# Gate rows of a dense PEER phase: groups of 16 blocks loaded in quarters, and the first eight blocks' rows of the third tile copied within SBUF

## The chip, the core and the metric

The kernel runs on one core of a Trainium2 chip. The metric is the device time of one execution in microseconds (us); before the change the median of 3 runs is 1922.52 us (1922.35 to 1923.98).

## What is computed

One inference step of a one-layer decoder on 576 tokens (512 of a prompt, 8 x 8 of a sample group) of width 1024: a mixer (an S5 state-space group and an RWKV-7 group), then PEER, a retrieval from 16384 experts of one neuron each. The change touches PEER alone:

```python
q = (xb @ w_q).reshape(PEER_BLOCK, PEER_HEADS, 2, PEER_HALF)
s1 = einsum('thd,hnd->thn', q[:, :, 0], k1); s2 = einsum('thd,hnd->thn', q[:, :, 1], k2)
v1, i1 = top_k(s1, 16); v2, i2 = top_k(s2, 16)
sc, pos = top_k(v1[..., :, None] + v2[..., None, :], 16)      # 8 heads x 16 experts per token
gate = softmax(sc)
act = gelu(einsum('thkd,td->thk', u_tab[idx], xb), approximate=False)
out = einsum('thk,thkd->td', gate * act, v_tab[idx])
```

## The kernel before

The tokens lie in five tiles, ORDER = (1, 2, 3, 0, 4); four have 128 tokens, tile 4 has 64. Each goes through front and back (the mixer, L1228 is its output projection), select (the queries, 64 matmuls `pas` with wq at L1268 in each half, and the products with the keys at L1284) and pick (the top-16 searches on DVE, L1304 to L1356). PEER's experts are then applied in two ways.

**Gathers, tiles 0 and 4.** POOL fetches each token's rows of u_tab and v_tab by indirect DMA (L1444, tile gr), DVE multiplies and adds (L1449 to scr, L1459 to acc). run() deals three such steps out to each dense block.

**Dense, tiles 1, 2 and 3 (384 tokens).** All 16384 experts are computed in 128 blocks of 128. For a block b, ublock() loads ur (512 KB), splits it into uh (ACT, L1512) and ul (DVE, L1513), and makes pd with 24 matmuls (L1516). dense() takes the Gelu of pd to wf (ACT, L1597), multiplies wf by the block's gate row (DVE, L1599), splits that into wh (ACT, L1602) and wl (DVE, L1603), loads vr (512 KB, L1611), splits it into vh (ACT, L1614) and vl (DVE, L1615), and adds into six PSUM banks with 18 matmuls po (L1619). dh and dl (L1551, L1552) are the split of the tokens, made once ahead.

**The gate rows.** For an expert that a token has not picked the gate is 0. gbuild(), woven with select and pick, makes the gate matrix for one dense tile in 8 steps of 16 tokens: for 4 tokens at a time (a group) two tiles ab are written (ACT L1490 and L1491 or DVE L1493; ACT L1496 or POOL L1498), four matmuls put their product into PSUM (L1501; par, pag, pah are the banks) and ACT copies that to Gst, 128 x 2048 (L1502). Gst is written to a buffer Gd in device memory, 1 MB for each of the 24 steps (L1504). From there loadG() in dense() (L1571) reads the rows of GBL = 8 blocks into a tile Gr, of which there are two: 16 tokens of 8 blocks are 512 bytes on end, so a load is 24 x 128 pieces of 512 bytes, 1.5 MB. There are 16 such loads.

All these loads and the writes of Gd are issued by SP, one after the other, on one queue; POOL's gathers are on another. The program is put in order by a scheduler ahead of time: each engine runs its instructions in a fixed order, and a DMA can be put ahead of where the code names it (issue_after).

Of the kernel before, what the change touches and what calls it, by code (L numbers as in the profile page):

```python
# [6 lines left out]
F32 = mybir.dt.float32  # L7
# [6 lines left out]
OP = mybir.AluOpType  # L14
# [164 lines left out]
class Kernel:  # L179
    DENSE = (1, 2, 3)  # L180
    ORDER = (1, 2, 3, 0, 4)
    TG = 16
    GBL = 8
    RATE = 3.0
    WS5, WAD, WS6, WA6, WD = 3.0, 0.0, 1.0, 1.0, 0.3
    PB = {"r": 3, "s": 3, "h": 1, "g": 1}
    UX, UWT, AB2 = 0, 0.5, 15
    UG = True
    UO = -100000
    PO, GO, SO, RO, FO = {}, {}, {4: 4000}, {}, {}  # L190
# [4 lines left out]
    GB = 5  # L195
# [1275 lines left out]
    def gbuild(self, d):  # L1471
        V, S, G, T, SY = self.nc.vector, self.nc.scalar, self.nc.gpsimd, self.nc.tensor, self.nc.sync
        iob = self.iota[:, None, :].to_broadcast([128, 4, 128])
        n = self.TG
        gp, nb = (self.gp2, self.AB2) if d == 2 and self.AB2 else (self.gp, self.AB)
        for tg in range(128 // n):
            Gst = self.gs.tile([128, 128, n], F32, name="Gst")
            for q in range(n // 4):
                t0 = d * 128 + tg * n + q * 4

                def bc(t):
                    return t[:, t0:t0 + 4, None].to_broadcast([128, 4, 128])
                oh = gp.tile([128, 128, 4], BF16, name="oh", bufs=self.OHB)
                B = gp.tile([128, 4, 128], F32, name="ab", bufs=nb)
                A = gp.tile([128, 4, 128], F32, name="ab", bufs=nb)
                self.gv = V.tensor_tensor(oh, self.io4, self.dib[:, None, t0:t0 + 4].to_broadcast([128, 128, 4]), op=OP.is_equal)  # L1486
                oh = oh.rearrange("p n t -> p t n")
                if q % 4 in self.BA:
                    for t in range(4):
                        S.activation(B[:, t], self.iota, AF.Abs, bias=self.dix[:, 0, t0 + t:t0 + t + 1], scale=-1.0)  # L1490
                    S.activation(B, B, AF.Relu, bias=1.0, scale=-1.0)  # L1491
                else:
                    self.gv = V.tensor_tensor(B, iob, bc(self.dix[:, 0]), op=OP.is_equal)  # L1493
                if q % 4 in self.AA:
                    for t in range(4):
                        S.activation(A[:, t], oh[:, t], AF.Copy, scale=self.dix[:, 1, t0 + t:t0 + t + 1])  # L1496
                else:
                    G.tensor_tensor(A, oh, bc(self.dix[:, 1]), op=OP.mult)  # L1498
                pg = self.ps([128, 4, 128], self.GR[d][(tg * n // 4 + q) % len(self.GR[d])])
                for t in range(4):  # L1500
                    T.matmul(pg[:, t, :], B[:, t, :], A[:, t, :], start=True, stop=True)  # L1501
                S.copy(Gst[:, :, 4 * q:4 * q + 4], pg.rearrange("p t n -> p n t"))  # L1502
                yield
            SY.dma_start(self.Gd[d * (128 // n) + tg], Gst.rearrange("p n t -> p (n t)"))  # L1504

    def ublock(self, b, pa, pool):
# [7 lines left out]
        for k in range(KB):  # L1514
            for i, (u, h) in enumerate(((uh, dh), (uh, dl), (ul, dh))):
                nc.tensor.matmul(pa, u[:, k, :], h[:, k, :], start=(k == 0 and i == 0), stop=(k == KB - 1 and i == 2))  # L1516

    def open_dense(self):
        S, V, SY = self.nc.scalar, self.nc.vector, self.nc.sync
        N = 128 * len(self.DENSE)  # L1520
        sc = self.sd = Scope(self.tc)
        kw = dict(reuse_waits="tile")
        dq = sc.pool("dq", **kw)
        self.ud = sc.pool("ud", **kw)
        if self.EU:
            self.ue = sc.pool("ue", **kw)
        if self.ED:
            self.dp = sc.pool("dp", 1, **kw)
        self.sh = Scope(self.tc)
        self.hf = self.sh.pool("hf", **kw).tile([128, KB, N], F32, name="hf")  # L1530
        if self.AB2:
            self.gp2 = self.sh.pool("gp2", **kw)
        ua = self.sh.pool("ua", **kw)
        self.ua = []
        for b in range(self.UX):
            t = ua.tile([128, KB, 128], F32, name="ua%d" % b)
            SY.dma_start(t, self.I["u_t"][b])
            self.ua.append(t)
        self.dh = dq.tile([128, KB, N], F32R, name="dh")
        self.dl = dq.tile([128, KB, N], F32R, name="dl")  # L1540
        self.wu = []
        for d, ti in enumerate(self.DENSE):
            sl = slice(128 * d, 128 * d + 128)
            SY.dma_start(self.hf[:, :, sl], self.h2d[ti].rearrange("p (k t) -> p k t", k=KB))

    def dense(self):
# [3 lines left out]
        N = 128 * nd  # L1550
# [15 lines left out]
                po = pso.tile([128, 512], F32, name="po%d%d" % (d, n))  # L1566
                outs.append(po)

        def loadG(g):
            t = dp.tile([128, N // TG, GBL, TG], F32, name="Gr", bufs=2)  # L1570
            SY.dma_start(t.rearrange("p g n t -> p g (n t)"),  # L1571
                         self.Gd[:, :, g * GBL * TG:(g + 1) * GBL * TG].rearrange("g p x -> p g x"))
            return t

        def first(b):
            if b < ux:
# [9 lines left out]

        with self.tc.issue_after(self.kld.ins):
            pa = first(0)
            G1 = loadG(0)
        for b in range(128):  # L1590
            if b % GBL == 0:
                Gr = G1
            if b % GBL == self.GPF and b + GBL < 128:
                with self.tc.issue_after(self.kld.ins):
                    G1 = loadG(b // GBL + 1)
            wf = pa if b < ux else dp.tile([128, N], F32, name="wf", bufs=2)
            S.activation(wf, pa, AF.Gelu)  # L1597
            w3 = wf.rearrange("p (g t) -> p g t", t=TG)
            V.tensor_tensor(w3, w3, Gr[:, :, b % GBL, :], op=OP.mult)  # L1599
            wh = dp.tile([128, N], F32R, name="wh", bufs=2)  # L1600
            wl = dp.tile([128, N], F32R, name="wl", bufs=2)
            S.copy(wh, wf)  # L1602
# [24 lines left out]
    def run(self, stop=None):  # L1627
# [48 lines left out]
        if stop == "mix":  # L1676
            weave(tc, (pk, 1.0, True))
        else:
            dense, gs = self.dense(), self.gathers()
            n = m = 0.0  # L1680
            for b, r in enumerate(dense):
                m += self.PW
                while m >= 1 and pk:
                    m -= 1
                    with tc.issue_after(self.gv.ins):
                        live = next(pk, 0)
                    if live == 0:
                        pk = None
                        self.sx.close()
                if b >= self.FB:  # L1690
                    if b == self.FB:
                        fl = self.open_finish()
                    with tc.issue_after(self.vld.ins):
                        next(fl, None)
                n += self.RATE * r * 128 / (128 - 0.5 * len(self.wu))
                with tc.issue_after(self.mark):
                    while n >= 1:
                        next(gs, None)
                        n -= 1
            for _ in gs:  # L1700
                pass
            self.sp.close()
            self.sf.close()
        if stop == "mix":
            self.sx.close()
            self.sh.close()
# [28 lines left out]
```

## Time and profile before

| | |
|---|---|
| median of 3 runs | 1922.52 us |
| the profiled execution, and its span | 1922.74 us, 1921.0 us |
| PE busy | 1772.8 us (92%) |
| DVE busy | 1508.1 us (79%) |
| ACT, POOL busy | 801.0 us (42%), 683.0 us (36%) |
| mean granted TensorE clock | 0.964 |
| share of the chain that ended last: PE | 62% |

The profile is of one execution. "Busy" is a share of the span; the chain of waits goes back from the last instruction to whatever released each step. The dense blocks begin at 804.5 us and the last block's po ends near 1898 us. Each block has 24 matmuls pd and 18 matmuls po.

### The profile page before, as it was taken

The page shows a single profiled execution, that of the slowest core. Times are in us where ns is not written, and L with a number is a line of the kernel's source. Part 1 is how long each engine was busy: PE and PEld are TensorE (multiplying, and loading weights), DVE is VectorE, ACT ScalarE, POOL GpSimd, SP SyncE. Part 2 cuts the span into 40 slices and gives each one's busy share as a digit, 9 for nine tenths or more (in the row PEclk, how much of TensorE's full clock was granted, in tenths as well). Part 3 has the DMA queues.
Part 4 walks back from the last instruction along what each step waited for, and adds up shares of the span by engine and source line. Part 5 has one row for each costly group of instructions (what it writes and reads, how often), then busy time and mean ns, then how long its engine had stood idle before and what let it go on. Part 6 is the DMA issues. An engine that isn't in the chain of part 4 may idle for free.

```text
span 1921.0 us, 32712 instructions
## 1 busy us (share of the span) xinstructions
PE 1772.8 (92%) x12299; PEld 1527.8 (80%) x12299; DVE 1508.1 (79%) x3073; ACT 801.0 (42%) x1466; POOL 683.0 (36%) x540
## 2 busy tenths in 40 slices
PE   8899987988879897889999999999999999999994
PEld 5699645757558676778999988899998999999993
DVE  7968324495996977789888877788888878888998
ACT  4232515535674677833333333433333333333332
POOL 0000101000351333334554444355445445444554
PEclk9999999989889898989999999999999999999998
DMA  8524654644345585589999998899999999999985
GB/s 328 159 87 105 202 179 145 205 138 151 122 150 195 193 296 210 221 297 333 370 340 340 350 356 313 295 374 342 343 355 317 347 340 343 331 342 349 331 318 190
DMA packets 203230, 513.82 MB, mean 267 GB/s; under 512 B 26232, under 2 KB 88824, under 8 KB 198976
## 3 DMA queue, kind: packets, MB, share of 16 engines
q1 hardware_dynamic: 147488, 309.34, 46.8%
q0 software_dynamic: 55584, 202.40, 28.7%
q8 instruction: 96, 1.57, 0.3%
q14 instruction: 62, 0.51, 0.1%
HBM read 470.89 MB, written 39.62 MB: 266 GB/s over the span
## 4 chain that ended last, share of the span: by engine, by line
PE 62%; DVE 10%; ACT 2%; DMA 1%; issue 1%; POOL 1%; POOLq 0%; DVEq 0%; ACTq 0%; SPq 0%
PE po L1619 27%; PE pd L1516 27%; PE pas L1268 3%; DVE oh L1486 1%; PE par L1501 1%; DVE ab L1493 1%; DMA Gr<-Gd 1%; PE pas L1228 1%; PE pag L1501 1%; PE pah L1501 1%; PE par L997 0%; DVE vals L1304 0%; DVE idxu L1305 0%; DVE idxu L1308 0%; DVE t2s L1306 0%
## 5 line engine op out<-in xcount | busy, mean ns | idle before, releaser
L1444 POOL DMA_INDIRECT gr<-v_tab,ei x192 | 261.0, 1359 | 274.6 <-DVE acc L1459 233.5
L1444 POOL DMA_INDIRECT gr<-u_tab,ei x192 | 251.6, 1310 | 274.0 <-DVE scr L1449 250.4
L1516 PE MATMUL pd<-dh,uh 128*128 128x384 f32 x1024 | 343.8, 336 | 4.8 <-ACT wf L1597 4.8
L1516 PE MATMUL pd<-dh,ul 128*128 128x384 f32 x1024 | 343.8, 336 | 0.0
L1516 PE MATMUL pd<-dl,uh 128*128 128x384 f32 x1024 | 343.2, 335 | 0.0
L1512 ACT CAST uh<-ur 128x1024 fp32r<-128x1024 f32 x128 | 134.5, 1050 | 276.7 <-PE pd L1516 264.3
L1459 DVE SCALAR_TENSOR_TENSOR acc<-gr,act,acc 128x1024 f32<-128x1024 f32 x190 | 243.2, 1280 | 2.3 <-DMA gr<-v_tab,ei 0.5
L1619 PE MATMUL po<-vl,wh 128*128 128x512 f32 x768 | 239.0, 392 | 0.6 <-DVE vl L1615 0.6
L1619 PE MATMUL po<-vh,wl 128*128 128x512 f32 x768 | 236.8, 390 | 0.0
L1449 DVE SCALAR_TENSOR_TENSOR scr<-gr,h 128x1024 bf16<-128x1024 f32 x192 | 235.1, 1224 | 1.4 <-DMA gr<-u_tab,ei 0.2
L1602 ACT CAST wh<-wf 128x384 fp32r<-128x384 f32 x128 | 65.8, 515 | 364.8 <-PE po L1619 348.0
L1513 DVE TENSOR_TENSOR ul<-ur,uh 128x1024 fp32r<-128x1024 f32 x128 | 156.5, 1223 | 78.2 <-ACT uh L1512 78.0
L1619 PE MATMUL po<-vh,wh 128*128 128x512 f32 x768 | 202.2, 398 | 15.2 <-ACT wh L1602 7.7
L1516 PEld LDWEIGHTS pd<-dh,uh 128*128 128x128 f32 x1024 | 192.3, 188 | 11.1 <-ACT wf L1597 5.8
L1516 PEld LDWEIGHTS pd<-dl,uh 128*128 128x128 f32 x1024 | 192.2, 188 | 6.0 <-issue 0.8
L1516 PEld LDWEIGHTS pd<-dh,ul 128*128 128x128 f32 x1024 | 192.1, 188 | 0.4
L1619 PEld LDWEIGHTS po<-vh,wh 128*128 128x128 f32 x768 | 141.8, 189 | 43.3 <-ACT vh L1614 12.8
L1615 DVE TENSOR_TENSOR vl<-vr,vh 128x1024 fp32r<-128x1024 f32 x128 | 156.2, 1220 | 22.0 <-ACT vh L1614 21.9
L1619 PEld LDWEIGHTS po<-vl,wh 128*128 128x128 f32 x768 | 144.5, 189 | 33.1 <-DVE vl L1615 1.4
L1619 PEld LDWEIGHTS po<-vh,wl 128*128 128x128 f32 x768 | 144.2, 188 | 31.2
L1498 POOL TENSOR_TENSOR ab<-oh,dix 128x512 f32<-128x512 bf16 x72 | 88.8, 1240 | 176.7 <-DVE oh L1486 68.9
L1614 ACT CAST vh<-vr 128x1024 fp32r<-128x1024 f32 x128 | 134.4, 1050 | 21.2 <-DMA vr<-v_tab 15.3
(471 smaller groups left out, 2976.2 us busy)
## 6 DMA issues: line engine op xcount, KB each, us to landing
ur<-u_t SPq DMA_DIRECT2D x128, 512.0 KB
vr<-v_tab SPq DMA_DIRECT2D x128, 512.0 KB
Gd<-Gst SPq DMA_DIRECT2D x24, 1024.0 KB
Gr<-Gd SPq DMA_DIRECT2D x16, 1536.0 KB
wo<-w_out SPq DMA_DIRECT2D x40, 512.0 KB
wq<-w_q SPq DMA_DIRECT2D x40, 512.0 KB
wt<-w_ada SPq DMA_DIRECT2D x32, 512.0 KB
wr<-w_in SPq DMA_DIRECT2D x18, 512.0 KB
```

The source lines that it names most:

```text
L1444: G.indirect_dma_start(out=r, out_offset=None, in_=I[tab], in_offset=bass.IndirectOffsetOnAxis(ap=ei[:, k:k + 1], axis=0))
L1449: V.scalar_tensor_tensor(scr, r, 1.0, h2, op0=OP.mult, op1=OP.mult, accum_out=act[:, k:k + 1])
L1459: V.scalar_tensor_tensor(acc, r, act[:, k:k + 1], acc, op0=OP.mult, op1=OP.add)
L1498: G.tensor_tensor(A, oh, bc(self.dix[:, 1]), op=OP.mult)
L1501: T.matmul(pg[:, t, :], B[:, t, :], A[:, t, :], start=True, stop=True)
L1512: nc.scalar.copy(uh, ur)
L1513: self.mark = nc.vector.tensor_tensor(ul, ur, uh.bitcast(F32), op=OP.subtract).ins
L1516: nc.tensor.matmul(pa, u[:, k, :], h[:, k, :], start=(k == 0 and i == 0), stop=(k == KB - 1 and i == 2))
L1602: S.copy(wh, wf)
L1614: S.copy(vh, vr)
L1615: V.tensor_tensor(vl, vr, vh.bitcast(F32), op=OP.subtract)
L1619: T.matmul(outs[2 * d + n], w[:, d * 128:(d + 1) * 128], v[:, n * 512:(n + 1) * 512], start=(b == 0 and i == 0), stop=(b == 127 and i == 2))
```

## The change

GBL goes from 8 to 16: a tile of gate rows now holds 16 blocks, so the 16 tokens of 16 blocks are 1024 bytes on end. Two large tiles, GA and GB, take turns (128 x 6144 numbers each). GA is opened before the third dense tile's gbuild, and the tiles ab of that gbuild go from 15 to 13. GB is opened when pick has ended. The first 16 blocks' rows are in GA, in two halves of 8 blocks. G0, blocks 0 to 7: for dense tiles 1 and 2 a DMA of 1 MB (in the first step of the third tile's gbuild), for the third tile 8 copies of 128 x 128 by DVE from Gst. G8, blocks 8 to 15: a load of 1.5 MB in 512-byte pieces. All later groups come in four loads of 6 x 128 pieces of 1024 bytes (768 KB).

```diff
-    GBL = 8
+    GBL = 16
-    UX, UWT, AB2 = 0, 0.5, 15
+    UX, UWT, AB2 = 0, 0.5, 13
...
                 S.copy(Gst[:, :, 4 * q:4 * q + 4], pg.rearrange("p t n -> p n t"))
                 yield
+            if d == 2:
+                V.tensor_copy(self.G0[:, d * (128 // n) + tg], Gst[:, 0:8, :])
+                if tg == 0:
+                    self.loadG(self.G0, 0, 8, 0, d * (128 // n))
             SY.dma_start(self.Gd[d * (128 // n) + tg], Gst.rearrange("p n t -> p (n t)"))
...
+    def loadG(self, t, b0, nb, g0, g1):
+        self.nc.sync.dma_start(t[:, g0:g1].rearrange("p g n t -> p g (n t)"),
+                               self.Gd[g0:g1, :, b0 * self.TG:(b0 + nb) * self.TG].rearrange("g p x -> p g x"))
...
+        self.GA = sc.pool("g0", 1, **kw).tile([128, N * self.GBL], F32, name="GA")
+        self.G0, self.G8 = (t.rearrange("p (g n t) -> p g n t", n=8, t=self.TG)
+                            for t in (self.GA[:, :8 * N], self.GA[:, 8 * N:]))
...
+        Gr, r0, plan = self.G0, 0, {2: (self.G8, 8, 8, 0, ng)}
...
             pa = first(0)
-            G1 = loadG(0)
         for b in range(128):
-            if b % GBL == 0:
-                Gr = G1
-            if b % GBL == self.GPF and b + GBL < 128:
+            if b == 8:
+                Gr, r0 = self.G8, 8
+            elif b and b % GBL == 0:
+                Gr, r0 = (GA, GB)[b // GBL % 2], b
+            if b == 11:
+                GB = self.GB_.rearrange("p (g n t) -> p g n t", n=GBL, t=TG)
+                for i in range(4):
+                    plan[11 + i] = GB, 16, GBL, ng // 4 * i, ng // 4 * (i + 1)
+            if b >= 16 and b % GBL == 0 and b + GBL < 128:
+                for i in range(4):
+                    plan[b + 2 + 2 * i] = (GA, GB)[(b // GBL + 1) % 2], b + GBL, GBL, ng // 4 * i, ng // 4 * (i + 1)
+            if b in plan:
                 with self.tc.issue_after(self.kld.ins):
-                    G1 = loadG(b // GBL + 1)
+                    self.loadG(*plan[b])
...
-            V.tensor_tensor(w3, w3, Gr[:, :, b % GBL, :], op=OP.mult)
+            V.tensor_tensor(w3, w3, Gr[:, :, b - r0, :], op=OP.mult)
```

Line numbers in the changed kernel are higher by 4 from gbuild's write on (Gd<-Gst L1508, ur L1513, uh L1516, pd L1520, loadG L1523), by 17 in dense() (wf L1614 and L1616, wh L1619, wl L1620, vr L1628, vh L1631, po L1636).

The change moves instructions. SP's order where the dense blocks begin, before:

```order
L1504 DMA Gd<-Gst 128x2048
L1509 DMA ur<-u_t 128x1024
L1571 DMA Gr<-Gd 128x24x128 x2
L1611 DMA vr<-v_tab 128x1024
L1509 DMA ur<-u_t 128x1024 x2
L1611 DMA vr<-v_tab 128x1024
```

and now (the first row stands earlier, between two loads of wq in the last tile's select; the second is the last write of Gd):

```order
L1523 DMA GA<-Gd 128x16x128
...
L1508 DMA Gd<-Gst 128x2048
L1513 DMA ur<-u_t 128x1024
L1523 DMA GA<-Gd 128x24x128
L1628 DMA vr<-v_tab 128x1024
L1513 DMA ur<-u_t 128x1024 x2
L1523 DMA GB<-Gd 128x6x256 x4
L1628 DMA vr<-v_tab 128x1024
```

Before, both first loads of gate rows stand behind the last write of Gd. Now only the second half of GA does, and the four quarters of GB follow three loads later, ahead of block 3's vr.

SP's order and, under it, ACT's order at the load that follows block 31's wf, before:

```order
L1611 DMA vr<-v_tab 128x1024
L1509 DMA ur<-u_t 128x1024
L1571 DMA Gr<-Gd 128x24x128
L1611 DMA vr<-v_tab 128x1024
L1509 DMA ur<-u_t 128x1024
```

```order
L1602 CAST wh<-wf 128x384
L1614 CAST vh<-vr 128x1024
L1597 ACTIVATE wf<-pd 128x384
L1512 CAST uh<-ur 128x1024
```

and now:

```order
L1628 DMA vr<-v_tab 128x1024
L1513 DMA ur<-u_t 128x1024
L1523 DMA GB<-Gd 128x6x256 x4
L1628 DMA vr<-v_tab 128x1024
L1513 DMA ur<-u_t 128x1024
```

```order
L1619 CAST wh<-wf 128x384
L1614 ACTIVATE wf<-pd 128x384
L1631 CAST vh<-vr 128x1024
L1516 CAST uh<-ur 128x1024
```

The four quarters, which the code names two blocks apart, stand in a row, with the next vr (block 31's) behind them. On ACT the Gelu of block 34 has moved ahead of block 31's vh; on PE, likewise, block 35's pd has moved ahead of block 31's po. Four quarters in a row stand behind block 31, 47, 63, 79 and 95; two and two stand behind blocks 7 and 15. At 47 PE's order is not turned in this way.

PE's order around the last tile's queries (pas<-t4s,wq) and key products, before:

```order
L1268 MATMUL pas<-t4s,wq 128x128 x32
L1501 MATMUL pag<-ab 128x128
L1268 MATMUL pas<-t4s,wq 128x128 x32
L1284 MATMUL pas<-keys,t4s 128x128 x8
L1501 MATMUL pag<-ab 128x128 x3
L1501 MATMUL par<-ab 128x128 x2
L1284 MATMUL pas<-keys,t4s 128x128 x8
L1501 MATMUL par<-ab 128x128 x2
```

and now:

```order
L1268 MATMUL pas<-t4s,wq 128x128 x32
L1501 MATMUL par<-ab 128x128 x4
L1501 MATMUL pag<-ab 128x128 x3
L1268 MATMUL pas<-t4s,wq 128x128 x8
L1501 MATMUL pag<-ab 128x128
L1501 MATMUL pah<-ab 128x128 x4
L1501 MATMUL par<-ab 128x128 x7
L1268 MATMUL pas<-t4s,wq 128x128 x24
L1284 MATMUL pas<-keys,t4s 128x128 x8
L1501 MATMUL par<-ab 128x128 x5
L1284 MATMUL pas<-keys,t4s 128x128 x8
```

Between the last key product and the first pd there were 90 matmuls of gbuild (22.5 groups of four); now there are 68 (17 groups), and the others stand among the queries. The split dh of the tokens on ACT and dl on DVE are also put later than before, dl into a pick.

## Rows read from the trace of the kernel before

**Rows 1.** The page: busy engines, DMA queues, and the chain's shares by line.

```profile
PE 1772.8 (92%) x12299; PEld 1527.8 (80%) x12299; DVE 1508.1 (79%) x3073; ACT 801.0 (42%) x1466; POOL 683.0 (36%) x540
q0 software_dynamic: 55584, 202.40, 28.7%
PE po L1619 27%; PE pd L1516 27%; PE pas L1268 3%; DVE oh L1486 1%; PE par L1501 1%; DVE ab L1493 1%; DMA Gr<-Gd 1%; PE pas L1228 1%; PE pag L1501 1%; PE pah L1501 1%; PE par L997 0%; DVE vals L1304 0%; DVE idxu L1305 0%; DVE idxu L1308 0%; DVE t2s L1306 0%
```

**Rows 2.** The chain, 688 to 857 us: start us, us, what.

```profile
688.70 2.64 ACT dh L1551
...
775.26 0.89 PE pag L1501 x8
...
804.77 1.09 ACT Gst L1502 x2
805.87 7.57 DMA Gd<-Gst
813.55 14.93 DMA Gr<-Gd
828.50 0.57 DVE wf L1599
829.15 0.52 ACT wh L1602
829.71 6.54 PE po L1619 x18
836.25 4.19 PE pd L1516 x24
840.44 4.12 PE po L1619 x18
844.56 4.18 PE pd L1516 x24
```

**Rows 3.** Windows: length, busy PE, PEld, DVE, ACT, POOL, clock, DMA share, GB/s.

```profile
774.00:804.50 30.50, 25.28 (x185) 23.93 (x183) 22.24 (x89) 29.51 (x78) 15.06 (x12) 0.89 0.53 213
810.00:820.00 10.00, 6.89 (x38) 6.58 (x39) 10.00 (x52) 3.13 (x4) 5.06 (x4) 1.00 0.73 223
820.00:830.00 10.00, 2.30 (x13) 1.98 (x12) 2.46 (x17) 0.85 (x2) 2.74 (x3) 0.70 1.05 398
830.00:840.00 10.00, 10.00 (x41) 8.68 (x41) 9.87 (x61) 4.74 (x8) 0.00 (x0) 0.78 0.77 266
840.00:850.00 10.00, 10.00 (x52) 8.99 (x51) 10.00 (x16) 5.38 (x7) 5.15 (x4) 1.00 0.81 263
870.00:880.00 10.00, 10.00 (x54) 9.27 (x53) 10.00 (x19) 4.13 (x6) 5.50 (x4) 1.00 0.93 316
```

**Rows 4.** Timelines of DVE (first row) and PE: start, us, work, idle before and releaser.

```profile
828.50 1.03 DVE L1599 TENSOR_TENSOR wf<-wf,Gr 128x384 f32<-128x384 f32 x2 [7.54 <-DMA Gr<-Gd]
829.71 1.22 PE L1619 MATMUL po<-vh,wh 128*128 128x512 f32 x2 [7.70 <-ACT wh L1602]
```

**Rows 5.** One DVE instruction of 128 x 128 numbers (ns: least, median, most).

```profile
L1315 DVE CAST i<-idxu x5: 169/214/218, 409.2 to 813.7; 128x128 f32<-128x128 uint32 x4, 128x64 f32<-128x64 uint32 x1
```

**Rows 6.** Timeline of SP: the vr behind three loads of gate rows.

```profile
879.23 7.05 SPq L1611 DMA_DIRECT2D vr<-v_tab  x1
944.24 7.92 SPq L1611 DMA_DIRECT2D vr<-v_tab  x1
1010.69 6.04 SPq L1611 DMA_DIRECT2D vr<-v_tab  x1
```

**Rows 7.** Timelines of ACT and PE: when these vr had come, and the next po.

```profile
894.03 1.05 ACT L1614 CAST vh<-vr 128x1024 fp32r<-128x1024 f32 x1 [2.55 <-DMA vr<-v_tab]
959.47 1.05 ACT L1614 CAST vh<-vr 128x1024 fp32r<-128x1024 f32 x1 [1.52 <-DMA vr<-v_tab]
1025.61 1.05 ACT L1614 CAST vh<-vr 128x1024 fp32r<-128x1024 f32 x1 [1.21 <-DMA vr<-v_tab]
895.41 0.39 PE L1619 MATMUL po<-vh,wh 128*128 128x512 f32 x1
961.87 0.63 PE L1619 MATMUL po<-vh,wh 128*128 128x512 f32 x2
1028.33 0.63 PE L1619 MATMUL po<-vh,wh 128*128 128x512 f32 x2
```

**Rows 8.** Waits of PE for vh, 828 to 1200 and 1200 to 1921 us: total, times, longest.

```profile
PE po L1619 <- ACT vh L1614: 3.8, 4, 1.1
PE po L1619 <- ACT vh L1614: 3.4, 3, 1.1
```

**Rows 9.** DMA at 1214:1221 (without gathers), 943:958 and 814:835: packets, MB, share.

```profile
DMA packets 3284, 2.26 MB, mean 322 GB/s; under 512 B 45, under 2 KB 3117, under 8 KB 3284
q1 hardware_dynamic: 3277, 2.24, 102.0%
...
q0 software_dynamic: 868, 3.16, 52.0%
...
q0 software_dynamic: 864, 3.15, 36.8%
```

More of the change, by code (lines that the diff above doesn't have):

```diff
@@ L1567, in dense @@
                 outs.append(po)
[L1569 to L1573, printed above, removed]
+        GA = self.GA.rearrange("p (g n t) -> p g n t", n=GBL, t=TG)
+        GB, ng = None, N // TG
+        Gr, r0, plan = self.G0, 0, {2: (self.G8, 8, 8, 0, ng)}
         def first(b):
@@ L1689, in run @@
                         self.sx.close()
+                        sg = Scope(tc)
+                        self.GB_ = sg.pool("gB", side="right", reuse_waits="tile").tile([128, 384 * self.GBL], F32, name="GB")
                 if b >= self.FB:
@@ L1703, in run @@
             self.sf.close()
+            sg.close()
         if stop == "mix":
```

## Prediction

> **What bounds the kernel now.** First the page [rows 1]: PE is busy for 92% of the span, and the chain of waits runs through po and pd for 27% each. Time is won only where PE stands still, or where its work begins late. The loads of gate rows hold 1% of the chain, so next comes the chain around the start of the dense blocks [rows 2]: the last Gst is ready at 805.87, its write to Gd takes 7.57 us, the first load of gate rows 14.93, and only then do wf, wh and block 0's po follow. The timelines say what that costs [rows 4]: DVE waits 7.54 us for the load, PE 7.70 us for wh. The windows say the same [rows 3]: PE works 2.30 of 10 us in 820 to 830. They show two more things. The granted clock falls to 0.70 and 0.78, a mix of its two levels 1.2 and 2.4 GHz, after PE had stood still; the first po takes 6.54 us, the next 4.12, so 2.42 us more are lost. And DVE is full in 810 to 820 and in 840 to 850 and 870 to 880: it has little to give but those 7.54 us.
>
> From then on PE is full, 4.18 us of pd and 4.12 of po for each block [rows 2]. What still stops it is vr behind a load of gate rows. In the three cases shown vr landed 14.8, 15.2 and 14.9 us after SP began to issue it, and ACT had waited 2.55, 1.52 and 1.21 us for it [rows 6, 7]; yet the next po began at its turn. The waits of PE for vh come to 3.8 + 3.4 = 7.2 us in seven cases [rows 8].
>
> **The change part by part.** The sum is made against the profiled execution, 1922.74 us (its span is 1921.0; the median of the runs is 0.22 us below, so the two are one).
>
> *gbuild's end: -2.5 us.* Between 774.0 and 804.5 ACT is busy for 29.51 of 30.5 us [rows 3]: with 22 to 23 groups there, one costs 1.34 us. Now 17 groups instead of 22.5 are left behind the last key product: 5.5 x 1.34 = 7.4 us less. But these 5.5 groups stand among the queries, where each takes PE 0.89 us [rows 2]: 4.9 us. Net -2.5. Bounds: -7 (if PE would have idled there) and +2 (two buffers fewer for ab; dl put into a pick; the SP queue held at the new load of tiles 1 and 2 until two writes of Gd have landed, at 7.57 us each). The split dh leaves a place where it stood on the chain with 2.64 us [rows 2] for one later on ACT; I count that as nothing, being only moved.
>
> *Block 0's gate row without the way through Gd: -9 us.* The third tile's rows now come from Gst by DVE, and those of tiles 1 and 2 are loaded long before. wf then waits for DVE alone, which came free 7.54 us before the load landed. po can start some 7.7 us earlier, right behind block 2's pd, and without the stop the clock should stay up: 2.42 us more, 10.1 in all. DVE, full in the windows that follow, moves forward by only 7.5; I take 9, between 5 and 10.
>
> *Eight copies: +0.8 us.* A copy of 128 x 128 is close to the cast of that size, 0.21 us [rows 5]: 1.7 us. About half of them stand in gbuild, beside ACT; the others where DVE is full. Bounds 0 and 1.7.
>
> *The first quarters of GB: +1 us.* 3 MB go ahead of block 3's vr. Before, 3 MB in two loads did about the same and drained in the 21 us of 814 to 835. By then PE is past its first two po; 0 to +4.
>
> *Five loads of 3 MB instead of ten of 1.5 MB: +0.5 us.* Here is the change's own price. A 512-byte piece takes 28.5 ns: 102.0% of 7 us on 16 engines, less 160 packets of 4 KB, over 3117 [rows 9]. A gather's packet, 3.64 KB in the mean, takes 28.7% x 1921 us x 16 / 55584 = 159 ns [rows 1]. A straight line through both gives 50 ns for 1024 bytes; the bounds are 45 (the gathers' rate) and 57 (the small pieces' rate). A load of 3072 pieces then takes an engine 192 x 50 = 9.6 us instead of 5.5: 4.1 more. Gathers run beside it, with 36.8% to 52.0% of the engines' time [rows 9]. In the double load of 814 to 835 the gathers gave way, so that 4.1 us would lengthen the drain by about as much; at the mean share it would be 4.1 / 0.556 = 7.4. I take 6, nearer to the shares of the steady blocks. vr's landing moves from 15.0 to 21.0 us after its issue. It is due, with 1.05 us for vh ahead of the next po, after 15.1, 16.6 and 16.6 us [rows 6, 7], 16.1 in the mean. So it is 4.9 us late. At four of the five loads PE now has one more pd ahead of that po, 4.18 us: 0.7 us is left of each; at block 47 all of it. 4 x 0.7 + 4.9 = 7.7, less the 7.2 us of old waits, is +0.5. The bounds of the time added, 3.1 / 0.63 = 4.9 and 5.4 / 0.48 = 11.3 us, give vr 3.8 to 10.2 us late, so -3 to +27. The loads of two quarters behind blocks 7 and 15 take 96 x 50 = 4.8 us, less than before: nothing.
>
> Here the Trainium skill speaks against the change. "DMA: Bandwidth & Descriptors", Specifications, gives 512 bytes as the least transfer for line rate, so that 1024 bytes would take twice the time of 512. The rows differ: a packet seven times as large as 512 bytes took 5.6 times as long.
>
> *The tail.* The last blocks and the gathers, three to a block, move together: nothing.
>
> Sum: -2.5 - 9 + 0.8 + 1 + 0.5 = -9.2, so 1913.5 us.
>
> **The rivals.**
> *A. The large loads cost more than the start gives (slower).* Without the five loads' stalls the sum stands at -2.5 - 9 + 0.8 + 1 - 7.2 = -16.9. Their stalls are 4 x (L - 4.2) + L, with L what vr is late, so from L = 6.7 us (7.8 us added) nothing is left, and from 7.5 us (8.6 added) the kernel is measurably slower. If bytes in 1024-byte pieces cost what they cost in 512-byte pieces, 57 ns, 5.4 us are added on an engine and 5.4 / 0.556 = 9.7 in the drain: L = 8.6, the stalls are 26.2 us, the time 1922.7 + 9.3 = 1932. For it: half of the bounds lie beyond 7.8, and loads that the code spaces two blocks apart stand in a row. Against it: the larger packets' better rate, and the pd put ahead. Twice the time of 512 bytes is what the line-rate rule of the Trainium skill's DMA page would make of it. Chance 0.22.
> *B. DVE takes the place of the wait (no change).* The key products of the last tile now come some 5 us later, and its pick, the copies and dl are all DVE's; if wf waits for DVE where it waited for the load, the start gives 3 us instead of 9, and gbuild's end nothing: 1922.7 - 3 + 0.8 + 1 + 0.5 = 1922. For it: the full windows of DVE [rows 3]. Against: 7.54 us of idle time that the new order opens to it. Chance 0.17.
> *C. The loads are hidden (faster still).* If the gathers give way as in the double load, 4.2 us are added: L = 3.1, under the pd put ahead, so 3.1 - 7.2 = -4.1; with a gbuild that ends 6 us earlier, 1922.7 - 6 - 9 + 0.8 + 1 - 4.1 = 1905.4. Chance 0.15.
>
> **How the numbers follow.** The forecast has 0.46. A measurement of this kernel can tell some 0.2% (3.8 us) from no change. Faster by more: the forecast and C, 0.61. Slower by more: A, 0.22. Within: B, 0.17. The range goes from 1904, just under C, to 1932, the middle of A; about 0.11 of A and 0.05 below or between are left out.
>
> **What would show it.** Right: DVE's wait for gate rows is gone from the list of waits, the first po follows block 2's pd with no gap of over 2 us and takes about 4.2 us, and the windows at 820 to 840 show PE full and the clock at 1.00. The chain holds no Gr and no Gd. PE's waits for vh appear at block 48 with about 5 us, and under 1 us at 31, 64, 79 and 95. gbuild's last matmul ends near 802. Wrong: waits of 4 us and more at all five loads (A); DVE named as what wh or po waits for at 815 to 830 (B); a gbuild that ends after 806.

## The result and the profile after

The change is slower. Its median is 1944.89 us (5 runs, 1935.03 to 1948.91), against 1923.98 for the kernel before, run alongside (5 runs, 1922.35 to 1926.21): a ratio of 1.0098, with a 95% interval of 1.0079 to 1.0117. The forecast, 1913.5 us, had the sign wrong, and its range ended at 1932. The profiled execution of the change took 1947.05 us with a span of 1945.3, 24.3 us more than before.

First the page of the kernel after: busy engines, and the chain's shares by engine and by line, as in [rows 1].

```profile
PE 1784.8 (92%) x12299; PEld 1529.3 (79%) x12299; DVE 1511.6 (78%) x3081; ACT 802.7 (41%) x1468; POOL 699.1 (36%) x540
...
PE 51%; DVE 12%; issue 6%; ACT 4%; POOL 3%; DMA 1%; POOLq 0%; SPq 0%; DVEq 0%; ACTq 0%
```

The work is the same; PE's share of the chain fell from 62% to 51%, so time went where PE waits. Where, the dense blocks tell when they are counted. The table says when as many of their matmuls had begun on PE as make 2, 10, 30, ... blocks (42 make one, so 84, 420, 1260, ...), from the first pd on, as a difference to before's profile in us. It is good to some 0.2 us.

| | first pd at | block 2 | 10 | 30 | 50 | 98 | 114 | end of the blocks |
|---|---|---|---|---|---|---|---|---|
| before, itself | 804.5 | 30.2 | 97.1 | 263.7 | 438.0 | 837.3 | 970.6 | 1094.0 |
| change | 810.6 | -6.4 | -4.4 | -4.7 | +2.7 | +6.4 | +20.4 | +19.0 |
| change again | 805.6 | -10.4 | -2.8 | -3.0 | +4.4 | +9.3 | +23.6 | +22.2 |
| spread | 815.6 | -10.4 | -6.2 | -6.6 | -4.0 | -3.4 | -3.9 | -3.4 |
| held before | 808.5 | -0.3 | -0.2 | -0.6 | -2.7 | -3.4 | -3.8 | -4.5 |
| held change | 803.5 | -10.3 | -3.2 | -3.4 | -4.6 | +4.2 | +3.8 | +2.4 |
| held spread | 801.1 | -10.4 | -6.5 | -6.9 | -7.4 | -7.8 | -8.2 | -8.0 |
| copies alone, held | 802.3 | -10.4 | -5.8 | -6.2 | -7.9 | -8.4 | -8.6 | -10.0 |
| no copies | 803.6 | +0.2 | +4.6 | +4.3 | +7.5 | +12.3 | +14.4 | +13.0 |
| no copies, held | 804.7 | -0.2 | +4.2 | +3.5 | +0.4 | +8.3 | +7.9 | +6.6 |
| two vh | 801.1 | -7.2 | -5.7 | -5.7 | -7.8 | -6.6 | -6.0 | -12.6 |
| late | 811.2 | -10.4 | -9.2 | -9.6 | -12.9 | -12.7 | -13.1 | -12.5 |
| late, 512 bytes | 802.8 | -5.9 | -5.9 | -6.3 | -11.8 | -12.4 | -12.8 | -13.6 |
| late, two vh | 807.2 | -7.1 | -6.9 | -7.1 | -12.1 | -13.0 | -13.4 | -19.8 |

The first two kernels answer to the prediction; the others are the experiments below. The start gained, then lost some of it by block 10; from block 30 to the end the change loses 23.7 us (25.2 in the second profile), 14 of them between blocks 98 and 114. The waits of PE after the start (828 to 1930; us in total, times, longest) stand for [rows 8]:

```profile
PE po L1636 <- ACT vh L1631: 20.0, 24, 1.6
...
PE po L1636 <- DVE vl L1632: 3.5, 1, 3.5
```

24 waits of at most 1.6 us, where 5 were expected. Most of them do not stand at the loads; of the five loads only the one at block 47, whose vr no pd covers, stops PE for long, 3.5 us at block 48's po, for vl. The timelines of SP and PE where the load behind block 95 goes out:

```profile
1625.74 10.86 SPq L1523 DMA_DIRECT2D GB<-Gd  x4
1636.70 3.77 SPq L1628 DMA_DIRECT2D vr<-v_tab  x1
...
1648.57 0.45 PE L1520 MATMUL pd<-dh,uh 128*128 128x384 f32 x1 [0.58 <-ACT wf L1614]
```

At the load PE waits 0.58 us, for a Gelu (wf) and not for vh: the pd that was put ahead covers vr's lateness, as the prediction had it. What comes after is in the chain of the kernel after, 1668 to 1687 us (start us, us, what):

```profile
1668.48 3.89 PE pd L1520 x22
1672.37 2.77 PE po L1636 x12
1675.15 0.02 issue
1675.17 1.05 ACT vh L1631
1676.22 0.04 issue
1676.27 1.64 PE po L1636 x6
1677.91 3.84 PE pd L1520 x22
1681.74 2.78 PE po L1636 x12
1684.52 0.02 issue
1684.54 1.05 ACT vh L1631
1685.60 0.04 issue
1685.64 1.64 PE po L1636 x6
```

PE's fixed order here has only 2 or 3 matmuls of pd between the last po of one block and the first of the next, thirteen times on end (behind blocks 97 to 109). And vh is one buffer: the next vh cannot be written before the last po has read this one. ACT's timeline has the other half of it:

```profile
1674.72 0.51 ACT L1619 CAST wh<-wf 128x384 fp32r<-128x384 f32 x1 [6.51 <-PE po L1636]
1675.17 1.05 ACT L1631 CAST vh<-vr 128x1024 fp32r<-128x1024 f32 x1
```

vh waits for no DMA (no bracket): vr had long landed. Its 1.05 us lie bare between two po. One thing more holds this vh, which is block 98's, to the same moment: ACT's order has block 99's wh ahead of it, and that wh (of which there are two) waits for block 97's po as well. From one vh to the next it is 1684.54 - 1675.17 = 9.37 us; before, a block took 4.19 + 4.12 = 8.31 [rows 2]. Windows of one stretch, 1690 to 1750, show the same (length, busy PE, PEld, DVE, ACT, POOL, clock, DMA share, GB/s). The kernel after:

```profile
1690.00:1750.00 60.00, 55.71 (x273) 48.19 (x271) 54.66 (x53) 18.39 (x26) 38.41 (x27) 1.00 0.96 344
```

and the kernel before:

```profile
1690.00:1750.00 60.00, 60.00 (x305) 54.55 (x304) 50.57 (x51) 21.83 (x30) 29.69 (x22) 1.00 0.95 341
```

PE began 273 instructions instead of 305 at the same clock of 1.00 and nearly the same DMA traffic.

What such a place costs can be read in every kernel with one vh, nearly always alike, from the start of the matmul ahead of it to the first po: 1.52 us where no pd lies between, 1.13 with two, 0.95 with three, 0.41 with six, and 0.17 to 0.23 where nothing is late. The kernel before has such places too, behind blocks 35, 37 and 39; its timelines of ACT and PE at block 38's po:

```profile
1155.21 1.04 ACT L1614 CAST vh<-vr 128x1024 fp32r<-128x1024 f32 x1
1156.31 1.65 PE L1619 MATMUL po<-vh,wh 128*128 128x512 f32 x6 [1.13 <-ACT vh L1614]
```

There too vh waits for no DMA.

### The profile page after: what moved, and what is told of

Same layout as the page of the kernel before. It is cut to its first block, busy times and chain, and to the rows that moved or that the text cites. A ratio compares the mean times of both kernels' runs of the same rounds, so it can differ in the third digit from the quotient of the medians.

```text
span 1945.3 us, 32730 instructions
## 1 busy us (share of the span) xinstructions
PE 1784.8 (92%) x12299; PEld 1529.3 (79%) x12299; DVE 1511.6 (78%) x3081; ACT 802.7 (41%) x1468; POOL 699.1 (36%) x540
## 4 chain that ended last, share of the span: by engine, by line
PE 51%; DVE 12%; issue 6%; ACT 4%; POOL 3%; DMA 1%; POOLq 0%; SPq 0%; DVEq 0%; ACTq 0%
PE pd L1520 23%; PE po L1636 22%; POOL gr L1444 3%; PE pas L1268 3%; DVE oh L1486 2%; DVE ab L1493 1%; ACT vh L1631 1%; DVE idxu L1305 1%; DVE idxu L1308 1%; DVE vals L1304 1%; PE par L997 1%; DVE t2s L1306 1%; DVE pk L1351 0%; DMA gr<-u_tab,ei 0%; DVE vals L1307 0%
## 5 line engine op out<-in xcount | busy, mean ns | idle before, releaser
L1444 POOL DMA_INDIRECT gr<-u_tab,ei x192 | 262.5, 1367 | 275.8 <-DVE scr L1449 231.0
L1444 POOL DMA_INDIRECT gr<-v_tab,ei x192 | 269.0, 1401 | 244.9 <-DVE acc L1459 209.1
L1520 PE MATMUL pd<-dh,uh 128*128 128x384 f32 x1024 | 346.0, 338 | 8.9 <-ACT wf L1614 8.9
L1520 PE MATMUL pd<-dh,ul 128*128 128x384 f32 x1024 | 345.3, 337 | 1.5 <-DVE ul L1517 1.5
L1520 PE MATMUL pd<-dl,uh 128*128 128x384 f32 x1024 | 344.5, 336 | 0.0
L1636 PE MATMUL po<-vl,wh 128*128 128x512 f32 x768 | 238.2, 391 | 3.5 <-DVE vl L1632 3.5
L1636 PE MATMUL po<-vh,wl 128*128 128x512 f32 x768 | 237.0, 390 | 0.0
L1619 ACT CAST wh<-wf 128x384 fp32r<-128x384 f32 x128 | 65.9, 515 | 397.2 <-PE po L1636 384.9
L1516 ACT CAST uh<-ur 128x1024 fp32r<-128x1024 f32 x128 | 134.3, 1049 | 229.5 <-PE pd L1520 224.6
L1636 PE MATMUL po<-vh,wh 128*128 128x512 f32 x768 | 202.0, 398 | 20.2 <-ACT vh L1631 20.0
L1520 PEld LDWEIGHTS pd<-dh,uh 128*128 128x128 f32 x1024 | 193.3, 189 | 19.1 <-ACT wf L1614 12.0
L1520 PEld LDWEIGHTS pd<-dl,uh 128*128 128x128 f32 x1024 | 193.2, 189 | 4.9
L1520 PEld LDWEIGHTS pd<-dh,ul 128*128 128x128 f32 x1024 | 193.1, 189 | 2.6 <-DVE ul L1517 2.3
L1636 PEld LDWEIGHTS po<-vh,wh 128*128 128x128 f32 x768 | 140.5, 188 | 52.5 <-ACT vh L1631 29.7
L1636 PEld LDWEIGHTS po<-vl,wh 128*128 128x128 f32 x768 | 143.7, 188 | 34.1 <-DVE vl L1632 4.3
L1636 PEld LDWEIGHTS po<-vh,wl 128*128 128x128 f32 x768 | 144.3, 188 | 31.2
L1631 ACT CAST vh<-vr 128x1024 fp32r<-128x1024 f32 x128 | 134.3, 1049 | 13.2 <-PE po L1636 7.1
```

Source lines behind the costliest of these rows:

```text
L1444: G.indirect_dma_start(out=r, out_offset=None, in_=I[tab], in_offset=bass.IndirectOffsetOnAxis(ap=ei[:, k:k + 1], axis=0))
L1516: nc.scalar.copy(uh, ur)
L1631: S.copy(vh, vr)
L1636: T.matmul(outs[2 * d + n], w[:, d * 128:(d + 1) * 128], v[:, n * 512:(n + 1) * 512], start=(b == 0 and i == 0), stop=(b == 127 and i == 2))
```

## The experiments

Every kernel computes the whole result. Three explanations were open after the result. **O**: the order that PE was given because of the loads. **D**: the loads themselves (3 MB in one piece of SP's queue, vr behind them). **S**: the start (13 buffers for ab instead of 15, the copies, a later dl).

**Spread.** Each quarter stands behind the v_tab load of the block before the one that names it, so that the four no longer stand in a row:

```diff
-                with self.tc.issue_after(self.kld.ins):
+                with self.tc.issue_after(self.vld.ins):
                     self.loadG(*plan[b])
```

> Edit: the quarter loads are tied to the vr load of the block ahead of them on SP's queue, so that they go out one by one as the code names them; else the change. The order now splits pd around po only at blocks 36 to 44. Theory O (PE's order: behind four quarters in a row the scheduler put a piece of pd ahead of po's first matmuls and kept that pattern; each such block loses about 0.9 us): 1921 us (1915 to 1927), no PE wait for vh at blocks 96 to 110. Rival D (the transfer itself: 3 MB ahead of vr): 1921 us as well, since the clump is gone. Rival S (the start: 13 buffers, copies, dl later): 1935 or more.

Measured: 1918.41 us (12 runs, 1913.88 to 1929.66), ratio 0.997 [0.9956, 0.9984]. Only the row of four is undone, and 26.5 us go. In the table the +23.7 after block 30 becomes +3.2. This rules out S, but not D, which expected the same.

**No copies.** The eight copies and the early load are out; the 8 blocks' rows are loaded after the last write of Gd, as before:

```diff
-            if d == 2:
-                V.tensor_copy(self.G0[:, d * (128 // n) + tg], Gst[:, 0:8, :])
-                if tg == 0:
-                    self.loadG(self.G0, 0, 8, 0, d * (128 // n))
...
             pa = first(0)
+            self.loadG(self.G0, 0, 8, 0, ng)
```

> Edit: the change without the copies and without the early load: block 0 to 7's rows of all three tiles go through Gd when the dense blocks begin, as before; groups of 16 in quarters as in the change. Its order splits pd at blocks 32 to 42 and at 64, 65, 80, 81, 96, 97. Theory O: the start as before (0), five loads with some 17 split blocks at 0.9 us, less the 5 us that before loses: 1932 us (1926 to 1938). Rival D: five loads at 3 to 5 us: 1940 to 1948. Rival S (the loss is made ahead of the dense blocks by the copies and dl): 1925 or less.

Measured: 1936.67 us (6 runs, 1933.83 to 1943.43), ratio 1.0073 [1.005, 1.0095]. At block 2 it stands at +0.2 where the change repeated has -10.4: the start's gain is the copies'. Yet as a whole it is faster than the change, since it loses 8.7 us after block 30 instead of 23.7: with another start the scheduler came to another order. The rows of four are the same here, and its order is uneven for eleven blocks behind block 31, but only for two each behind 63, 79 and 95. So the rows bring uneven places, and how long they go on hangs on the rest of the program.

**Held change.** The loads stay as they are, but pd of block b may not be put ahead of the last po of block b - 4, so PE's order keeps one pd and one po by turns:

```diff
+        with ExitStack() as st:
+            if b >= 4:
+                st.enter_context(self.tc.issue_after(self.pl[b - 4]))
-        for k in range(KB):
+            for k in range(KB):
...
-                        T.matmul(outs[2 * d + n], ...
+                        last = T.matmul(outs[2 * d + n], ...
+            self.pl.append(last.ins)
```

> Edit: the change with its clumped loads, but each block's pd is held on PE behind the last po of the block four before it, so that pd and po take turns whole. Theory O: the loss at blocks 96 to 110 (14 us) is gone, short waits for vh at the five loads take its place: 1926 us (1920 to 1932). Rival D: without the pd put ahead each of five loads costs 4 to 6 us more than it did: 1950 or more. Rival S: 1938 or more.

Measured: 1923.99 us (12 runs, 1918.52 to 1931.11), ratio 1.0001 [0.9986, 1.0017]. The same bytes, the same rows of four, and 21 us less, where D expected 1950 or more. Now the loads do stop PE where they stand. PE and ACT of the held change behind blocks 31 and 95, timelines:

```profile
1093.49 1.63 PE L1639 MATMUL po<-vh,wh 128*128 128x512 f32 x6 [2.54 <-ACT vh L1634]
...
1637.10 1.69 PE L1639 MATMUL po<-vh,wh 128*128 128x512 f32 x6 [2.37 <-ACT vh L1634]
...
1636.00 1.04 ACT L1634 CAST vh<-vr 128x1024 fp32r<-128x1024 f32 x1 [0.74 <-DMA vr<-v_tab]
```

and the same window as above:

```profile
1690.00:1750.00 60.00, 60.00 (x304) 54.45 (x303) 54.80 (x55) 20.70 (x29) 32.48 (x25) 1.00 0.94 336
```

304 instructions: PE is full again. Counted as in the table, but against the held spread below and from three blocks ahead of each load to six behind it, the five loads cost it 2.8, 1.7, 2.9, 2.4 and 4.2 us, 14.0 together.

**Held before.** The same hold on the kernel before, to see what the hold gives by itself:

> Edit: the kernel before with the same hold of pd behind po. It splits pd at blocks 35 to 41 and at each load, some 8 blocks in all. Theory O: these cost 3 to 5 us, so 1918 us (1916 to 1921). Rivals D and S: 1922 to 1924, as before.

Measured: 1922.54 us (12 runs, 1916.55 to 1930.31), ratio 0.999 [0.9974, 1.0007]. Not told apart from nothing in the medians, though its profile ends the blocks 4.5 us earlier: theory O had expected 3 to 5 us here and missed. The hold's 21 us in the change are not a gain that any kernel would have.

**Held spread.** Both edits, of the spread and of the held change:

> Edit: quarters one by one (as in the first run) and pd held behind po (as in the second). Theory O: nothing is left of split pd, and 12 to 15 us of PE's waits for vh behind four quarters are gone against the held change: 1916 us (1913 to 1920). Rival D (the loads cost by their bytes, wherever they stand): as the held change, 1922 to 1926.

Measured: 1917.11 us (8 runs, 1911.75 to 1923.07), ratio 0.9962 [0.9944, 0.998]. Against the held change 7 us in the medians and 10.4 in the table: that is the price of the rows of four themselves, once the order is even. (The 10.4 are the 14.0 of the five loads and some 3 at the first quarters of GB, less what the held spread loses elsewhere, for one 1.51 us at each of three po near block 38, where ACT has vh behind a Gelu.)

**Copies alone, held.** The copies and the early load, the hold, and for all else the loads of before: 8 blocks at a time in the halves of GA, 512-byte pieces, no GB:

```diff
-            if b == 8:
...
+            if b and b % 8 == 0:
+                Gr, r0 = (self.G0, self.G8)[b // 8 % 2], b
+            if b % 8 == self.GPF and b + 8 < 128:
                 with self.tc.issue_after(self.kld.ins):
-                    self.loadG(*plan[b])
+                    self.loadG((self.G0, self.G8)[(b // 8 + 1) % 2], b // 8 * 8 + 8, 8, 0, ng)
...
```

> Edit: the copies and the early load alone. Groups of 8 blocks in 512-byte pieces as before, in the two halves of GA, no GB; 13 buffers; pd held behind po. Against the held kernel before it differs by the start alone. Theory O with the start worth 6 us (block 4's pd waits for ur behind the load of the second half of GA): 1917 us (1914 to 1920). Rival S (13 buffers, copies and dl eat it ahead of the dense blocks): 1922 to 1925. Rival F (the start gives the 9 us forecast): 1913.

Measured: 1912.47 us (6 runs, 1910.5 to 1914.97), ratio 0.9935 [0.9921, 0.995]. The start gave what rival F said, not the 6 us of theory O: with the hold, this half of the change alone gives what the forecast gave the whole. Against it the held change loses 12.4 us by the table, of which 2.6 at the first quarters of GB (block 10) and 9.8 at the five loads.

**No copies, held.** The other half: large loads, no copies, the hold:

> Edit: groups of 16 in clumped quarters without the copies (as in the fourth run), pd held behind po. Against the held change it differs by the copies and the early load alone. Theory O with the start worth 6 us: 1929 us (1926 to 1933). Rival S: 1922 to 1925.

Measured: 1928.17 us (12 runs, 1923.76 to 1934.37), ratio 1.0018 [1.0004, 1.0032]. The large loads alone make the kernel slightly slower (0.18%, an interval just clear of 1), and against 1936.67 the hold takes off 8.5 us; by the table what is lost after block 30 falls from 8.7 to 3.1.

**Late.** The start held one more loss: from block 2 to 10 the held change gives back 7.1 of its 10.3 us, the held spread 3.9. ACT's wait there, in the timeline of the held spread:

```profile
831.22 1.04 ACT L1516 CAST uh<-ur 128x1024 fp32r<-128x1024 f32 x1 [7.42 <-DMA ur<-u_t]
```

This ur stands on SP behind the 1.5 MB of blocks 8 to 15. So that load moves behind block 3's vr, in the held spread:

```diff
-        Gr, r0, plan = self.G0, 0, {2: (self.G8, 8, 8, 0, ng)}
+        Gr, r0, plan = self.G0, 0, {4: (self.G8, 8, 8, 0, ng)}
```

> Edit: as the run with quarters one by one and pd held, and the load of blocks 8 to 15 is put behind block 3's vr, so that block 4's ur no longer stands behind it. If that load is what takes back 4 us of the start: 1912 us (1909 to 1916), and ACT's wait of 7.8 us for ur at block 4 is gone. If DVE, full there, is what takes it back: as the run without this edit, 1916.

Measured: 1912.61 us (6 runs, 1908.16 to 1917.37), ratio 0.9927 [0.9911, 0.9942]. The waits of ACT, 812 to 860, of this kernel:

```profile
ACT uh L1516 <- PE pd L1523: 12.5, 5, 4.4
ACT wh L1622 <- DVE wf L1619: 7.8, 4, 4.1
...
ACT vh L1634 <- DMA vr<-v_tab: 0.6, 1, 0.6
```

No wait for ur is left, and -9.2 us stand at block 10 instead of -6.5.

**Late, 512 bytes.** As late, but 8 blocks at a time in two halves, each behind a vr: 24 x 128 pieces of 512 bytes where late has 1024:

```diff
...
+            if (b == 4 or b >= 8 and b % 8 in (2, 4)) and b + 8 < 128:
+                g0, g1 = (0, ng) if b == 4 else (0, ng // 2) if b % 8 == 2 else (ng // 2, ng)
+                with self.tc.issue_after(self.vld.ins):
+                    self.loadG((self.G0, self.G8)[(b // 8 + 1) % 2], b // 8 * 8 + 8, 8, g0, g1)
...
```

> Edit: as the run with blocks 8 to 15 loaded late, quarters one by one and pd held, but with groups of 8 blocks: each load is two halves of 12 x 128 pieces of 512 bytes (768 KB) behind vr loads, in the two halves of GA, no GB. It differs from that run by the pieces' size alone. If larger pieces matter (rival P: 28.5 us of engine time in 1024-byte pieces against some 33 in 512-byte ones over 32 blocks): 1915 or more. If only the places of the loads and PE's order matter (theory O): the same within 0.2%, 1910 to 1915.

Measured: 1914.16 us (8 runs, 1911.27 to 1920.59), ratio 0.9949 [0.9933, 0.9966]. The intervals of the two overlap: once no more than 768 KB stand ahead of a vr, the size of the pieces, and with it the second large tile, can't be told from nothing. In both profiles DVE's last step of the gathers (acc) ends after PE, at 1898.5 against 1883.8 with 512 bytes and at 1897.1 against 1893.3 with 1024, so the medians could hide a small gain of PE; but in the table the blocks end 1.1 us earlier with 512. (At the prices measured below, 48.0 and 28.5 ns a piece, 32 blocks take an engine 18.4 us in 1024-byte pieces and 21.9 in 512-byte ones, less than the expectation says.)

**Change again.** The changed kernel itself, for a second profile:

> Edit: none, the change once more, on the chip of the run beside it. Theory O: the loss sits in the fixed order, so it recurs: 1940 to 1948 us, and PE waits for vh in each block from 98 to 110 again, 0.6 to 1.2 us. If the loss of the first profile was an accident of that execution (a low clock, a slow transfer), some of these blocks run without the wait and the time is under 1935.

Measured: 1944.6 us (6 runs, 1941.21 to 1945.3), ratio 1.01 [1.0082, 1.0119]. The waits of PE for vh between 1650 and 1800 are 13 with 8.9 us (and one of 0.8 at the same kind of place, put down to "issue"); in the first profile 14 with 9.6. So O holds: the loss sits in the fixed order.

**Two vh.** The change with one word more, a second buffer for vh:

```diff
-            vh = up.tile([128, D], F32R, name="vh", bufs=1)
+            vh = up.tile([128, D], F32R, name="vh", bufs=2)
```

> Edit: the change with a second buffer for vh, nothing else. vh then need not wait for the last matmul of the block ahead, so two po back to back should cost PE nothing. Its order still puts a pd ahead behind blocks 31, 63, 79 and 95, with some 15 split or doubled places from block 33 on. Theory O with its mechanism (one vh buffer, so that wh and vh stand bare between two po): 1922 to 1928 us, and few waits of PE for vh at those places. If a split pd costs by itself (weights loaded anew, or otherwise), or if the loads are what costs: 1934 or more.

Measured: 1914.04 us (10 runs, 1910.28 to 1920.05), ratio 0.9956 [0.9941, 0.997]: 31 us under the change, with its loads in their rows of four (three and one behind block 47), and 8 us under what theory O expected. The waits of PE, 828 to 1930, the whole list:

```profile
PE pd L1520 <- ACT wf L1614: 2.9, 5, 0.6
PE pd L1520 <- ACT uh L1516: 1.4, 1, 1.4
PE pd L1520 <- DVE ul L1517: 0.6, 1, 0.6
```

vh is gone from it. The scheduler made PE's order anew here as well: behind the last load it is out of turn for about two blocks and then goes 24 pd, 18 po again. But its order has 14 other places with at most six pd between two po, and there PE does not wait; timeline of PE behind block 5, with no pd between:

```profile
868.31 0.61 PE L1636 MATMUL po<-vh,wl 128*128 128x512 f32 x2
868.76 1.52 PE L1636 MATMUL po<-vh,wh 128*128 128x512 f32 x6
```

The first po begins 0.17 to 0.23 us after the matmul ahead of it at all 14, where one vh made 1.52 to 0.41; with one vh, by those prices, they would have cost some 13 us (an estimate). Such a place is therefore free once vh is ready. Two more things came with the buffer. ACT's order has the next block's wh ahead of vh in 11 blocks instead of 124. And the vr are fetched earlier: behind a row of four stands block 33's vr where the change has block 31's, sent out 10.9 to 14.0 us ahead of its po at four of the five rows, where the held change has 8.3 to 8.9; so the loads' own price is gone with the rest. This run doesn't part the buffer from these two: in ACT's old order wh would still have held vh.

**Late, two vh.** Late and the second buffer:

> Edit: the run with the late load of blocks 8 to 15, quarters one by one and pd held, with a second buffer for vh. Theory O: little is left for it to take, since pd and po take turns there: 1908 to 1913 us against 1912.6. If single buffering costs in every block: under 1905.

Measured: 1912.94 us (6 runs, 1912.08 to 1913.41), ratio 0.9944 [0.9928, 0.996]. By the table PE is 7.3 us earlier at the end of the blocks than in late, yet the time is the same: PE ends at 1881.9 of a span of 1911.4, and the gathers of the last tile are then last.

**The faster version** that came of it: late, 1912.61, 0.7% under before (copies alone, held; two vh; and late with two vh lie within 1.5 us of it, and are not told apart).

## Why the prediction was wrong

**The step that failed** is the cover in "Five loads of 3 MB instead of ten": "At four of the five loads PE now has one more pd ahead of that po, 4.18 us: 0.7 us is left of each". The term, +0.5 us, came out as +23.7 and +25.2 in the change's two profiles. The cover works at the load (PE waits 0.58 us there, for wf), but the pd put ahead is a pd that isn't there later. The prediction looked at the order at the loads and not at the blocks that follow, fifteen or so behind the last of them, where po of two blocks then stand nearly side by side and the single vh is bare each time, 0.9 us or so to a block: 14 us there, the rest behind the other loads and 3.5 at the uncovered one. Shown by two runs: the hold alone, which makes the order even, gives 21 us, and the second vh, with what came along, 31. That a bare vh costs the time is read from the chain and from the places with two vh, where it costs nothing; that the uneven order comes with the rows of four, from the spread, where the loads alone were moved and the long stretch went (a short one near block 40 stays, as in the kernel before).

**The old waits** were misread in the same term. It takes off 7.2 us, the waits of PE for vh in the kernel before [rows 8], as if vr behind the loads had made them. In none of the seven does vh wait for a DMA: they stand behind blocks 3, 35, 37 and 39 and between the last four blocks, where no pd or two lie between two po. The trace of before thus showed the very loss that sank the change; three of the seven, 3.4 us, stay in every kernel with one vh. Without the 7.2 the sum is 1920.7, no change that could be measured.

**The loads' own price** is the second part of that term. With the order held, vr costs PE 2.8 us at each load in the mean, where 4.9 were forecast without cover; but at all five loads, 14.0 us. Against the loads of before with the copies and the hold (copies alone, held) the table has +9.8 from block 10 on. So rival A, 1932 us with L = 8.6, had the side right and the mechanism wrong: vr was less late than forecast, not more, and the loss came of the order, not of the price of a byte.

**The price of a piece** was nearly right. DMA of the kernel after at 1229:1237, between gathers:

```profile
DMA packets 2758, 2.88 MB, mean 360 GB/s; under 512 B 60, under 2 KB 2719, under 8 KB 2758
q1 hardware_dynamic: 2758, 2.88, 104.6%
```

8 us x 16 x 1.046, less 39 packets at 159 ns, over the 2659 left between 512 bytes and 2 KB: 48.0 ns each, forecast 50 (47.0 over all 2719 under 2 KB, the way the prediction counted its 28.5). By the line-rate rule of the Trainium skill ("DMA: Bandwidth & Descriptors", Specifications) it would have been 57, twice the 512-byte piece's 28.5 [rows 9]; this trace doesn't bear that out: per byte the larger piece is some 16% cheaper.

**Block 0's gate row**, -9 (10.1 before the cut for DVE): -10.3 to -10.4 at block 2 in six of the ten profiles of kernels with the copies, the change's second among them. In the other four, its first among them, it is -5.9 to -7.2: there PE waited 4.00 to 5.27 us for wf at the second pd (2.76 in each of the six), and the granted clock of a window of 5 us behind it is 0.51 to 0.66, where the change's second profile has 1.00. The timeline of PE in the kernel after:

```profile
819.00 0.69 PE L1520 MATMUL pd<-dh,uh 128*128 128x384 f32 x1 [4.00 <-ACT wf L1614]
...
827.50 0.44 PE L1520 MATMUL pd<-dh,uh 128*128 128x384 f32 x1 [1.35 <-ACT wf L1614]
...
831.08 0.63 PE L1636 MATMUL po<-vh,wh 128*128 128x512 f32 x2
```

The first po has no bracket: it follows pd at once, as forecast, where [rows 4] show 7.70 us. Rival B, DVE in the place of the wait, did not come: wh waits for DVE there (1.23 us in the first profile, 3.04 in the second), but PE has pd meanwhile.

**A wait that was not counted** took some of it back. SP's queue in the kernel after:

```profile
820.26 0.38 SPq L1523 DMA_DIRECT2D GA<-Gd  x1
822.84 4.48 SPq L1628 DMA_DIRECT2D vr<-v_tab  x1
827.37 1.30 SPq L1513 DMA_DIRECT2D ur<-u_t  x2
831.14 13.04 SPq L1523 DMA_DIRECT2D GB<-Gd  x4
844.28 2.79 SPq L1628 DMA_DIRECT2D vr<-v_tab  x1
```

The load of blocks 8 to 15 went out in one, ahead of block 4's ur, while PE now ran 10 us earlier. Before, 3 MB stood on SP at this place, and PE stood still for the first half of them [rows 4]. ACT's wait for that ur is 7.4 us in the held spread; moving the load gives 2.7 us back at block 10 (late), a quarter of the gain.

**The first quarters of GB**, +1 (0 to +4): +2.6 by the held change against copies alone held, +3.3 against the held spread.

**gbuild's end**, -2.5 (-7 to +2): nothing came. From the write of tile 0's h2d (L1249) to the first pd it is 141.4 us before, 141.2 after, and between 140.2 and 143.0 in the others. The clause that failed is that the groups put among the queries cost only 4.9 us there. The last product with the keys, in the chains of before and after:

```profile
772.76 1.64 PE pas L1284 x16
787.65 1.64 PE pas L1284 x16
```

The write stood at 663.1 and 669.4, so this product ends 111.3 and 119.9 us behind it: 8.6 later, more than the 7.4 that 5.5 groups fewer were to save.

**The copies**, +0.8: they are 8 of 0.219 us in the median ([rows 5] have 0.214). Three of them stand in the chain of the kernel after, with 0.77 us, and five in the change's second profile, with 1.02; as forecast:

```profile
796.16 0.14 DVE GA L1505
798.60 0.15 DVE GA L1505
807.06 0.48 DVE GA L1505
```

**The sum.** The first pd comes 6.1 us late in the first profile (4.8 of it in a stretch told below), the blocks are 19.0 us longer, the tail 0.8 shorter: 24.3. In the second profile 1.1 + 22.2 - 0.8 = 22.5, the span's 1943.5 - 1921.0; the medians' difference is 20.9. Forecast: -2.5, -6.7 and 0.

**Left open.** Whether the held before's 4.5 us in the profile is a gain (its medians don't show one), and how much of the two vh's gain is the buffer, how much PE's order and ACT's order that came with it, and how much the earlier vr. What the gathers at the end would allow, were they shorter, was not tried.

## What to carry to other kernels

A late transfer that is covered by work pulled forward can be paid for afterwards: look at the order of the blocks behind it, and at each single buffer between two engines, whose refill is bare as soon as its two users stand side by side. Loads that the code spaces out may stand in one row on the queue; tie each to the transfer that it may not delay. Before a wait is charged to a load, see what the waiting operand itself waited for: here it was the matmuls, not the DMA. A start that comes earlier can turn the next load on the same queue into its bound, so cost the transfers behind it against the new times.

## What was not expected of the hardware

TensorE's clock differed where the program does not. Up to 670 us both kernels' instructions stand in the same order on PE, yet in 580 to 590 us the windows differ (columns as above). The kernel before:

```profile
575.00:580.00 5.00, 5.00 (x29) 4.65 (x29) 4.51 (x9) 4.69 (x12) 3.17 (x4) 0.67 0.29 117
580.00:585.00 5.00, 5.00 (x64) 4.68 (x64) 3.38 (x8) 4.19 (x12) 1.31 (x2) 1.00 0.65 227
585.00:590.00 5.00, 5.00 (x68) 4.69 (x67) 0.00 (x0) 0.72 (x2) 0.00 (x0) 1.00 0.72 221
```

and the kernel after:

```profile
580.00:585.00 5.00, 5.00 (x35) 4.76 (x36) 2.78 (x6) 4.84 (x14) 1.69 (x3) 0.50 0.51 210
585.00:590.00 5.00, 5.00 (x35) 4.66 (x35) 1.32 (x3) 0.00 (x0) 0.00 (x0) 0.56 0.27 68
```

From 580 on full clock, 2.4 GHz, in the one, and nearly all of the 10 us at 1.2 in the other, with half of the matmuls; some 4.8 us came of it, and stayed up to the first pd. In twelve of the fourteen profiles the clock is low for some 7 us somewhere between 553 and 580, in this one and the spread's for 17. The spread's shows 0.50 in both windows from 580; the eleven other experiments show 1.00 in both. A single profile's difference of 5 us is therefore no part of a change until a second one has it. And by the run of 512-byte pieces against 1024, halving the number of pieces bought nothing that could be measured once the loads were spread.
